# An encoder trunk on one core: the MLP's up product also in Strassen's 2x2 blocks, with its sums of weights formed beside the attention

## Chip, core and metric

One Trainium2 chip, one core. The metric is the device time of one execution in microseconds (us). The kernel computes in float32; products run on TensorE in `float32r` (named fp32r in the rows), where each operand is written as a high part plus a low part and three matmuls (high·high, high·low, low·high: `PASSES`) stand for one exact product.

## What is computed

Two layers over x (1024 tokens by 1024). The attention half of a layer has four groups of heads; the change is in the MLP half and in what stands beside the attention:

```python
h = _rmsnorm(x, norm2_g[l])
u = _dwconv3(h @ w_up[l], conv_w[l], conv_b[l])    # 1024 -> 2 x 2816, a width-3 convolution over the tokens
gate, val = u[..., :D_FF], u[..., D_FF:]
x = x + (jax.nn.silu(gate) * val) @ w_down[l]      # 2816 -> 1024
```

## The kernel before

**Planner and orders.** Python emits the program; a planner then orders every engine's instructions by a timeline of its own. SyncE (SP) issues all DMAs, in one queue. Only in the attention stream is TensorE's order written by hand: `stream` walks numbered positions p (B heads 0 to 63, C 64 to 127, D 128 to 159, A 160 to 223), each with one `step` (L490 splits its transposed probabilities), and calls `fill(p)` to interleave other work: the rest of the input projection up to about p = 55, then `switch` opens the pools of the residual, then output projections of finished head groups (`out_stage`), and at p = 190 pools are closed. `ld` (L438) fetches a head's q, k and v from DRAM some positions ahead, into three buffers.

**MLP up.** The normalised, transposed input lies split in `h2T[0]` and `h2T[1]` (tokens 0 to 511 and 512 to 1023; high and low part; eight chunks of 128 of the inner dimension). The 44 column chunks of `w_up` go in 22 pairs j (gate chunk j, value chunk 22 + j). `load` fetches a chunk of 128x1024 (`rawu`), ScalarE writes its high part, GpSimd its low part (`split`, L132/L136). `product` runs 8 x 3 x 2 = 48 matmuls of 128 columns by 512 tokens into a PSUM tile `u`, so a pair takes 96. `conv` then reads `u` from PSUM: one pass on ScalarE (L939), two on VectorE (L940, L941); `gate` applies silu on ScalarE and multiplies on GpSimd (L948, L952). The first eight products go to DRAM (`gd`), the rest stay in SBUF.

**MLP down.** It is already done by Strassen's seven block products per 2x2 blocks (`DOWN` lists, for each product, the blocks of A = gated values and of B = `w_down` that are added or subtracted, and where the result goes). Each product has 11 steps of 12 matmuls of 512 columns; VectorE forms the sum of A (L1052), `split` makes its two parts, and at the end of a product VectorE adds four PSUM banks into the residual `xacc` (L1061), once for each of 12 uses in all. `prep_down` forms the 77 operands of B for a layer while up runs: two loads, for 55 of them a sum on GpSimd (L1013), a split on ScalarE and VectorE (`wd`), and a store of 512 KB to DRAM (`bd`), from which `down` reads them.

Of the kernel before, what the change touches and what calls it, by code (L numbers as in the profile page):

```python
# [87 lines left out]
GD = 8  # L88


class K:
# [821 lines left out]
    def mlp(self, l, h2T, mp, gd, bd):  # L913


        nc, a = self.nc, self.a
        cw = mp.tile([128, 4, 2 * NFF], F32, tag="cw", name="cw", bufs=1)
# [4 lines left out]
        def load(jj):  # L922
            raw = self.raw.tile([128, KC, 128], F32, tag="raw", name="rawu")
            nc.sync.dma_start(raw, a["w_up"][l, jj])
            w = mp.tile([128, 2, KC, 128], F32R, tag="wu", name="wu", bufs=2)
            self.split((w[:, 0], w[:, 1]), raw, "act", "pool")
            return w

        def product(u, w, halves):
            i = 0  # L930
            for k in range(KC):
                for x, y in PASSES:
                    for n in halves:
                        self.mm(u[:, n * 512:(n + 1) * 512], w[:, x, k, :], h2T[n][:, y, k, :], i == 0, i == 23)
                    i += 1

        def conv(jj, u):
            c = mp.tile([128, S], F32, tag="c", name="c", bufs=3)
            nc.scalar.activation(c, u, AF.Identity, scale=cw[:, 1, jj:jj + 1], bias=cw[:, 3, jj:jj + 1])  # L939
            nc.vector.scalar_tensor_tensor(c[:, 1:], u[:, :S - 1], cw[:, 0, jj:jj + 1], c[:, 1:], op0=ALU.mult, op1=ALU.add)  # L940
            nc.vector.scalar_tensor_tensor(c[:, :S - 1], u[:, 1:], cw[:, 2, jj:jj + 1], c[:, :S - 1], op0=ALU.mult, op1=ALU.add)  # L941
            return c

        def gate(j, us):
            g, v = us
            nc.scalar.activation(g, g, AF.Silu)
            if j < GD:
                nc.gpsimd.tensor_tensor(v, v, g, op=ALU.mult)  # L948
                nc.sync.dma_start(gd[j * 128:(j + 1) * 128, :], v)
                return None  # L950
            t = gp.tile([128, S], F32, tag=f"g{j}", name="gg")
            nc.gpsimd.tensor_tensor(t, v, g, op=ALU.mult)  # L952
            return t.rearrange("p (a c) -> p a c", a=2)

        ws = [load(jj) for jj in (0, NFF)]
        yield
        uu = []
        for w in ws:
            uu.append(self.psS.tile([128, S], F32, tag="S", name="u0"))
            product(uu[-1], w, (0,))  # L960
            yield
        for u, w in zip(uu, ws):
            product(u, w, (1,))
        gs = [gate(0, [conv(jj, u) for jj, u in zip((0, NFF), uu)])]
        gp, pm = yield
        prep = self.prep_down(l, gp, bd)
        for j in range(1, NFF):
            us, w = [], []
            for jj in (j, NFF + j):
                w.append(load(jj))  # L970
                us.append(pm.tile([128, S], F32, tag="u", name="u", bufs=2))
                if j < NFF - 1:
                    product(us[-1], w[-1], (0, 1))
                    us[-1] = conv(jj, us[-1])
                next(prep, None)
                next(prep, None)
            if j == NFF - 1:

                for n in (1, 0):
                    for i in range(2):  # L980
                        product(us[i], w[i], (n,))
                us = [conv(jj, u) for jj, u in zip((j, NFF + j), us)]
            gs.append(gate(j, us))
        yield gs

# [10 lines left out]
    )  # L998

    ORDER = tuple(range(GD // 2, NFF // 2)) + tuple(range(GD // 2))  # L1000

    def prep_down(self, l, gp, bd):

        nc, a = self.nc, self.a
        for n, (_, Bs, _) in enumerate(self.DOWN):
            for c in self.ORDER:
                raw = gp.tile([128, 2, 512], F32, tag="rd", name="rawd", bufs=2)
                for q, (k, j, _) in enumerate(Bs):
                    r0 = (2 * c + k) * 128
# [363 lines left out]
```

## Time and profile before

| | |
|---|---|
| median of 3 runs | 3126.66 us (3122.52 to 3126.93) |
| the profiled execution | 3122.59 us, its span 3120.8 us |
| busy, share of the span | TensorE 95%, weight loads 82%, VectorE 65%, ScalarE 48%, GpSimd 34% |
| DMA | 437.5 MB, mean 140 GB/s |

All rows below come from that one execution. PE is TensorE, DVE is VectorE, ACT is ScalarE, POOL is GpSimd, SPq is SyncE's queue of DMAs. A line number as L132 is that of `split`, a helper, so such rows are told apart by their tiles. Layer 0 runs to about 1570 us, its attention stream from about 200 to 905, its up product to about 1345, its down product to about 1555; layer 1 has the same stages about 1550 us later.

### The profile page before, as it was taken

The numbers are of one execution on the slowest core, as the hardware profiler recorded it, in microseconds if no ns is written. First come the engines' busy times: TensorE is split into PE (matmuls) and PEld (weight loads), VectorE is DVE, ScalarE is ACT, GpSimd is POOL, SyncE is SP. The second block draws the span as 40 slices with busy tenths as digits, with TensorE's granted clock in tenths as the row PEclk, the third lists the DMA queues.
The fourth block names the chain that finished last, engine by engine and source line by source line (L and its number), as shares of the span: only waits on it lengthen the run. The fifth ranks groups of instructions, "written<-read, shape, count | busy, mean of one in ns | idle before, by whom it ended". The sixth has DMA issues, their size and how long they took to land. (4 is left out here: it accounts for less than half of the span.)

```text
span 3120.8 us, 45434 instructions
## 1 busy us (share of the span) xinstructions
PE 2965.2 (95%) x16536; PEld 2551.4 (82%) x16536; DVE 2017.8 (65%) x3366; ACT 1508.5 (48%) x2873; POOL 1049.8 (34%) x902
## 2 busy tenths in 40 slices
PE   7989899899999999999999899998999999999999
PEld 5978888788878888888889788887888788888887
DVE  6778887777744555344666898777777445552455
ACT  5557665766633333222344676657666333332221
POOL 2266410320144554421223653103202445443211
PEclk9999999999999999999999999999999999999999
DMA  4332231332267766355623312313213677662655
GB/s 142 114 105 74 58 122 51 77 73 62 25 221 263 247 231 219 134 211 190 220 96 123 101 54 69 124 45 86 75 45 49 236 272 250 226 214 89 236 193 185
DMA packets 357519, 437.51 MB, mean 140 GB/s; under 512 B 206128, under 2 KB 251568, under 8 KB 357296
## 3 DMA queue, kind: packets, MB, share of 16 engines
q1 hardware_dynamic: 357296, 434.61, 43.8%
q8 instruction: 131, 2.15, 0.3%
q14 instruction: 92, 0.75, 0.1%
HBM read 292.97 MB, written 131.07 MB: 136 GB/s over the span
## 5 line engine op out<-in xcount | busy, mean ns | idle before, releaser
L143 PE MATMUL u<-h2T,wu 128*128 128x512 f32 x4224 | 979.4, 393 | 5.3 <-DVE c L941 5.2
L143 PEld LDWEIGHTS u<-h2T,wu 128*128 128x128 f32 x4224 | 793.0, 188 | 190.1 <-issue 6.9
L143 PE MATMUL pj<-w,hT 128*128 128x256 f32 (+2 forms) x3072 | 488.3, 312 | 21.8 <-ACT w L136 9.6
L143 PEld LDWEIGHTS pj<-w,hT 128*128 128x128 f32 x3072 | 438.5, 194 | 47.2 <-ACT w L136 10.8
L132 DVE TENSOR_TENSOR wd<-rawd,wd 128x512 fp32r<-128x512 f32 x154 | 233.0, 1518 | 233.7 <-ACT wd L136 233.2
L489 ACT CAST PT<-pt 128x512 fp32r<-128x512 f32 x448 | 261.4, 583 | 180.8 <-PE pt L147 172.0
L490 DVE TENSOR_TENSOR PT<-pt,PT 128x512 fp32r<-128x512 f32 x448 | 304.7, 684 | 44.5 <-ACT PT L489 41.9
L147 PE MATMUL pt<-cst,P 128*128 128x128 f32 x1792 | 277.9, 278 | 50.6 <-DVE PT L490 45.0
L940 DVE SCALAR_TENSOR_TENSOR c<-u,cw,c 128x1023 f32<-128x1023 f32 x88 | 112.8, 1282 | 282.7 <-ACT c L939 282.7
L132 POOL TENSOR_TENSOR wu<-rawu,wu 128x1024 fp32r<-128x1024 f32 x88 | 215.1, 2446 | 218.9 <-ACT wu L136 209.7
L143 PEld LDWEIGHTS ot<-PT,v 128*128 128x128 f32 x1664 | 256.9, 193 | 32.2
L147 PEld LDWEIGHTS pt<-cst,P 128*128 128x128 f32 x1792 | 208.8, 142 | 84.1 <-issue 34.2
L143 PE MATMUL ot<-PT,v 128*128 128x256 f32 x1664 | 272.6, 287 | 0.0
L136 ACT CAST wd<-rawd 128x512 fp32r<-128x512 f32 x154 | 95.0, 621 | 348.4 <-POOL rawd L1013 271.8
L1013 POOL TENSOR_TENSOR rawd<-rawd 128x512 f32<-128x512 f32 x110 | 159.6, 1451 | 272.2 <-DMA rawd<-in_w_down_dram 260.5
L939 ACT ACTIVATE c<-u,cw 128x1024 f32<-128x1024 f32 x88 | 106.1, 1206 | 272.1 <-PE u L143 271.9
L143 PE MATMUL d<-h2T,ga 128*128 128x512 f32 x1008 | 230.9, 390 | 0.0
L143 PE MATMUL S<-k,q 96*128 96x512 f32 (+2 forms) x512 | 209.8, 435 | 17.9 <-DVE nmb L655 16.6
L143 PEld LDWEIGHTS d<-h2T,ga 128*128 128x128 f32 x1008 | 189.3, 188 | 40.3
L143 PE MATMUL od<-wo,mT 128*128 128x512 f32 x768 | 200.3, 400 | 0.9 <-DVE mT L1091 0.7
L143 PE MATMUL du<-h2T,ga 128*128 128x512 f32 x792 | 181.4, 390 | 0.0
L143 PEld LDWEIGHTS du<-h2T,ga 128*128 128x128 f32 x792 | 148.7, 188 | 31.7
(216 smaller groups left out, 4529.7 us busy)
## 6 DMA issues: line engine op xcount, KB each, us to landing
bd<-wd SPq DMA_DIRECT2D x154, 512.0 KB, 3.4
h2T<-bd SPq DMA_DIRECT2D x150, 512.0 KB, 3.2
rawd<-in_w_down_dram SPq DMA_DIRECT2D x264, 256.0 KB, 5.1
rawu<-in_w_up_dram SPq DMA_DIRECT2D x88, 512.0 KB, 4.6
rawi<-in_w_in_dram SPq DMA_DIRECT2D x20, 512.0 KB, 3.9
rawo<-in_w_out_dram SPq DMA_DIRECT2D x16, 512.0 KB, 3.3
gd<-c SPq DMA_DIRECT2D x16, 512.0 KB, 5.4
h2T<-gd SPq DMA_DIRECT2D x16, 512.0 KB, 6.8
```

What stands on the lines that cost most here:

```text
L132: eng.tensor_tensor(dst[1], src, dst[0].bitcast(F32), op=ALU.subtract)
L136: self.nc.scalar.copy(dst, src)
L143: self.nc.tensor.matmul(out, l, r, start=start, stop=stop)
L147: self.nc.tensor.transpose(out, in_, self.ident[:p, :p])
L489: nc.scalar.copy(PT[:, 0, :], pt)
L490: nc.vector.tensor_tensor(PT[:, 1, :], pt, PT[:, 0, :].bitcast(F32), op=ALU.subtract)
L939: nc.scalar.activation(c, u, AF.Identity, scale=cw[:, 1, jj:jj + 1], bias=cw[:, 3, jj:jj + 1])
L940: nc.vector.scalar_tensor_tensor(c[:, 1:], u[:, :S - 1], cw[:, 0, jj:jj + 1], c[:, 1:], op0=ALU.mult, op1=ALU.add)
L1013: nc.gpsimd.tensor_tensor(raw[:, 0], raw[:, 0], raw[:, 1], op=ALU.add if Bs[1][2] > 0 else ALU.subtract)
```

## The change

Pairs 3 to 20 of the up product (18 of 22) are done as one 2x2 by 2x2 block product each: rows gate and value, inner dimension in two halves of 512, tokens in two halves. Seven products of 12 matmuls replace eight. Each product of a pair gets a PSUM bank of its own, and VectorE adds the seven banks into two SBUF tiles `g` and `v`, which `conv` now reads from SBUF. Three sums of blocks of the input (`T1`, `T2`, `T4`) are formed in new tiles and one (`T3`) in the place of a quarter of `h2T[1]`, whose contents are put in DRAM (`hd`) first and read back before the last pair.

The weight sums are formed by a new generator `prep`, called from `fill` once per position from p = 66 on, in 91 jobs per layer: 36 for `w_up` (GpSimd adds and subtracts: 1 for an X job, 3 for a Y job, and two stores of 512 KB per pair, `sd`) and 55 for `w_down` (one GpSimd operation, one store of 256 KB, `bd`). `prep_down` and its splits are gone: `down` loads the sums, or `w_down` itself, unsplit and splits them on the spot. The gated products of pairs 0 to 19 all go to DRAM (`gd`); twelve come back into the T tiles, eight into `h2T[1]`.

```diff
-GD = 8
+UP7 = (3, NFF - 1)
...
+    def prep(self, l, pp, sd, bd):
...
+        jobs = [("XY"[i], j) for j in range(UP7[0], UP7[1]) for i in range(2)]
+        jobs += [(n, c) for n, (_, Bs, _) in enumerate(self.DOWN) if len(Bs) > 1 for c in self.ORDER]
...
+            t[i] = pp.tile([128, 2, 512], F32, tag="pw", name="pw", bufs=4)
...
+                nc.sync.dma_start(t[i], a["w_up"][l, jj].rearrange("p (h k) c -> p h (k c)", h=2))
...
+            if kind == "X":
+                G.tensor_tensor(r[:, 0], r[:, 0], r[:, 1], op=ALU.add)
+            elif kind == "Y":
+                x = t[i - 1]
+                G.tensor_tensor(r[:, 0], x[:, 0], r[:, 0], op=ALU.subtract)
+                G.tensor_tensor(x[:, 1], x[:, 1], r[:, 0], op=ALU.subtract)
+                G.tensor_tensor(r[:, 1], r[:, 1], r[:, 0], op=ALU.subtract)
+                nc.sync.dma_start(sd[j, 0], x)
+                nc.sync.dma_start(sd[j, 1], r)
+            else:
+                G.tensor_tensor(r[:, 0], r[:, 0], r[:, 1], op=ALU.add if self.DOWN[kind][1][1][2] > 0 else ALU.subtract)
+                nc.sync.dma_start(bd[kind][j], r[:, 0])
+        for i in range(len(jobs) + 2):
+            if i >= 2:
+                work(i - 2)
+            if i < len(jobs):
+                load(i)
+            yield
...
+        def operand(f, low):
+            w = mp.tile([128, 2, 4, 128], F32R, tag="wu", name="wu", bufs=6)
+            self.split((w[:, 0], w[:, 1]), f, "act", low)
+            return w
...
+        T1, T2, T4 = (tp.tile([128, 2, 4, 512], F32R, tag=f"T{i}", name=f"T{i}") for i in (1, 2, 4))
+        T3 = h2T[1][:, :, 0:4, :]
+        B11, B21, B22 = h2T[0][:, :, 0:4, :], h2T[0][:, :, 4:8, :], h2T[1][:, :, 4:8, :]
+        nc.sync.dma_start(hd, T3.bitcast(F32))
...
+        def sums(k):
+            f = [mp.tile([128, 2, 512], F32, tag="u", name="bf", bufs=2) for _ in range(2)]
+            b11, b12, b22, b21 = f[0][:, 0], f[0][:, 1], f[1][:, 0], f[1][:, 1]
+            for d, t in ((b11, B11), (b12, T3), (b22, B22), (b21, B21)):
+                join(d, t, k)
+            V.tensor_tensor(b11, b12, b11, op=ALU.subtract)
+            V.tensor_tensor(b22, b22, b11, op=ALU.subtract)
+            G.tensor_tensor(b21, b21, b22, op=ALU.subtract)
+            for t, d, eng in ((T1, b11, "dve"), (T2, b22, "dve"), (T4, b21, "pool")):
+                self.split((t[:, 0, k, :], t[:, 1, k, :]), d, "act", eng)
...
+        plain(1, load(1), (0, 1))
+        sums(0)
+        sums(1)
+        plain(2, load(2), (1, 0))
+        sums(2)
+        sums(3)
+        for k in range(4):
+            sums3(k)
...
+            w11 = operand(rg[:, 0:4, :], "pool")
+            s2 = operand(ry[:, 0:4, :], "dve")
+            s1 = operand(rx[:, 0:4, :], "pool")
+            w12 = operand(rg[:, 4:8, :], "dve")
+            s3 = operand(rx[:, 4:8, :], "pool")
+            s4 = operand(ry[:, 4:8, :], "pool")
+            w22 = operand(rv, "pool")
...
+            g, v = (mp.tile([128, S], F32, tag="u", name="u", bufs=2) for _ in range(2))
+            m1 = prod(bank(), w11, B11)
+            nc.scalar.copy(g[:, lo], m1)
+            V.tensor_tensor(v[:, lo], g[:, lo], prod(bank(), s2, T2), op=ALU.add)
+            V.tensor_tensor(g[:, hi], v[:, lo], prod(bank(), s1, T1), op=ALU.add)
+            V.tensor_tensor(g[:, lo], g[:, lo], prod(bank(), w12, B21), op=ALU.add)
+            p = pm.tile([128, S], F32, tag="u", name="X2", bufs=2)
+            m7 = prod(p[:, lo], s3, T3)
+            V.tensor_tensor(v[:, hi], g[:, hi], m7, op=ALU.add)
+            V.tensor_tensor(v[:, lo], v[:, lo], m7, op=ALU.add)
+            V.tensor_tensor(g[:, hi], g[:, hi], prod(p[:, hi], s4, B22), op=ALU.add)
+            p = pm.tile([128, S], F32, tag="u", name="X2", bufs=2)
+            V.tensor_tensor(v[:, lo], v[:, lo], prod(p[:, lo], w22, T4), op=ALU.add)
+            gs = [gate(j, (g, v))]
...
+        ws = load(NFF - 1)
+        nc.sync.dma_start(T3.bitcast(F32), hd)
+        back = [t[:, i, 2 * m:2 * m + 2, :].bitcast(F32) for t in (T1, T2, T4) for i in range(2) for m in range(2)]
...
-    def prep_down(self, l, gp, bd):
...
+                self.split((m[:, 0], m[:, 1]), r, "act", "pool")
...
-                self.split((w[:, 0], w[:, 1]), t[0], "act", "pool" if i % 3 == 1 else "dve")
+                self.split((w[:, 0], w[:, 1]), t[0], "act", "dve")
...
+                if 66 <= p < 190:
+                    adv("prep", 1)
```

`sums3(k)` forms `T3` in place: two joins on VectorE, a subtraction on GpSimd, a split whose low part alternates between GpSimd and VectorE. `prod` is 4 x 3 matmuls into one bank. `plain` is a pair as before, with the token halves one after the other.

## Rows read from the trace of the kernel before

**Rows 1.** Stretches: busy us of each engine (x instructions), granted clock, DMA share, GB/s.
```profile
950.00:1300.00 350.00, 350.00 (x1518) 284.50 (x1517) 178.08 (x125) 118.61 (x138) 180.56 (x92) 1.00 0.68 231
1350.00:1550.00 200.00, 200.00 (x876) 164.09 (x875) 109.93 (x148) 47.46 (x79) 37.09 (x28) 1.00 0.63 223
408.00:640.00 232.00, 212.14 (x1435) 187.25 (x1435) 176.19 (x358) 154.51 (x346) 41.55 (x31) 0.99 0.32 87
```

**Rows 2.** Chain that ended last, layer 1's MLP: start us, us, what, matmuls.
```profile
2417.81 11.03 PE u L143 x48
...
2493.29 411.39 PE u L143 x1776
2904.68 29.92 PE d L143 x132
```

**Rows 3.** Waits of TensorE, whole span: us in total, times, longest.
```profile
PE u L143 <- DVE c L941: 5.2, 3, 2.5
```

**Rows 4.** Groups by form: busy us, mean ns of one, idle before, releaser.
```profile
L941 DVE SCALAR_TENSOR_TENSOR c<-u,cw,c 128x1023 f32<-128x1023 f32 x88 | 112.8, 1282 | 3.0
L132 DVE TENSOR_TENSOR w<-raw,w 128x512 fp32r<-128x512 f32 x16 | 10.7, 695 | 1.1 <-ACT w L136 0.9
L1061 DVE TENSOR_TENSOR xacc<-xacc,d 128x512 f32<-128x512 f32 x56 | 35.1, 679 | 9.9 <-PE d L143 9.9
L136 ACT CAST wd<-rawd 128x512 fp32r<-128x512 f32 x154 | 95.0, 621 | 348.4 <-POOL rawd L1013 271.8 <-DMA rawd<-in_w_down_dram 74.8 <-issue 1.6
L939 ACT ACTIVATE c<-u,cw 128x1024 f32<-128x1024 f32 x88 | 106.1, 1206 | 272.1 <-PE u L143 271.9
```

**Rows 5.** VectorE's instructions in order of time, up stage: start us, us, what.
```profile
1062.95 2.26 DVE L132 TENSOR_TENSOR wd<-rawd,wd 128x512 fp32r<-128x512 f32 x1 [0.85 <-ACT wd L136]
1068.46 0.69 DVE L132 TENSOR_TENSOR wd<-rawd,wd 128x512 fp32r<-128x512 f32 x1 [3.26 <-ACT wd L136]
...
1071.89 1.28 DVE L941 SCALAR_TENSOR_TENSOR c<-u,cw,c 128x1023 f32<-128x1023 f32 x1
1073.64 2.25 DVE L132 TENSOR_TENSOR wd<-rawd,wd 128x512 fp32r<-128x512 f32 x1 [0.46 <-ACT wd L136]
```

**Rows 6.** GpSimd's instructions in the same time.
```profile
1062.21 2.44 POOL L132 TENSOR_TENSOR wu<-rawu,wu 128x1024 fp32r<-128x1024 f32 x1
...
1071.66 1.29 POOL L1013 TENSOR_TENSOR rawd<-rawd 128x512 f32<-128x512 f32 x1 [3.88 <-DMA rawd<-in_w_down_dram]
1072.91 2.44 POOL L132 TENSOR_TENSOR wu<-rawu,wu 128x1024 fp32r<-128x1024 f32 x1
1075.30 1.75 POOL L1013 TENSOR_TENSOR rawd<-rawd 128x512 f32<-128x512 f32 x1
1077.01 2.41 POOL L952 TENSOR_TENSOR gg<-c 128x1024 f32<-128x1024 f32 x1
```

**Rows 7.** Stretch 1352 to 1360, columns as in rows 1.
```profile
1352.00:1360.00 8.00, 8.00 (x37) 6.56 (x36) 5.36 (x5) 4.72 (x7) 1.31 (x1) 1.00 1.02 413
```

**Rows 8.** VectorE's L490 alone (one per position) by stretch: busy us (x times).
```profile
408.00:640.00 232.00, 62.72 (x93) 0.99 0.32 87
640.00:840.00 200.00, 52.81 (x78) 0.99 0.19 51
```

**Rows 9.** DMA issues, 404 to 424 us: times, KB each, median us to landing.
```profile
xacc<-in_x_dram SPq DMA_DIRECT2D x8, 512.0 KB, 7.5
...
ld<-sC SPq DMA_DIRECT2D x1, 256.0 KB, 6.8
```

**Rows 10.** DMA issues, 408 to 640 us.
```profile
ld<-sC SPq DMA_DIRECT2D x3, 256.0 KB, 3.5
```

**Rows 11.** DMA issues on the page: loads of the weights.
```profile
rawd<-in_w_down_dram SPq DMA_DIRECT2D x264, 256.0 KB, 5.1
rawu<-in_w_up_dram SPq DMA_DIRECT2D x88, 512.0 KB, 4.6
```

**Rows 12.** Line 1010 (loads of `prep_down`) in layer 0: first and last start.
```profile
L1010 SPq DMA_DIRECT2D rawd<-in_w_down_dram x132: 328/472/1311, 867.7 to 1268.1; - x132
```

## Forecast

> **What bounds the kernel now.** I read the page's shares first, then the stretches, because a share is a mean over stages. In the up stretch and in the down stretch TensorE is busy for the whole of the time, at a granted clock of 1.00 (2.4 GHz), while VectorE is busy for about half and GpSimd for half and a fifth [rows 1]. The chain says the same from its end: it is nothing but matmuls from the up product to the last step [rows 2]. Of all the waits of TensorE, the up product's longest group is 5.2 us in the whole span, three waits for VectorE to free PSUM [rows 3]. So a matmul less in up is time less, unless the work that replaces it becomes the bound; and the sums, splits and stores of `prep_down`, which run beside it, cost nothing today, so that taking them out of up gains nothing by itself. The stretch 408 to 640 us is most of C and D of the attention, where the new sums will run: TensorE is busy 212 of 232 us, VectorE 176, GpSimd 42, and the DMA engines 0.32 [rows 1].
>
> **Change, part by part.** The sum is made against the profiled execution, 3122.6 us; the median of the runs is 4 us above it, and I forecast the median by the same offset, rounded. A difference under 0.2% is about what cannot be told from no change.
>
> *Matmuls.* A pair goes from 96 to 84, so 36 pairs lose 432. The chain has 411.39 us for 1776 in up, 231.6 ns each, and 29.92 us for 132 in down, 226.7 ns [rows 2]. Up alternates two banks with the token halves; the new `prod` stays in one bank with the three passes of down's form. The second half of the first pair already runs one token half at a time: 11.03 us for 48, 229.8 with the drain of the last in it. So I take 226.7: 36 x (96 x 0.2316 - 84 x 0.2267) = 36 x (22.23 - 19.04) = -115. Two more pairs per layer get separate halves: 4 x 96 x 0.0049 = -2. If the form does not matter, it is -432 x 0.2316 = -100. Both ends stay for the range.
>
> *What else a new pair asks of the engines in its 19.04 us.* ScalarE: seven casts of 0.62, two conv passes of 1.21, silu at most as much, one copy at most a cast: 4.3 + 2.4 + 1.2 + 0.6 = 8.5 [rows 4]. VectorE: seven adds with one PSUM operand at 0.68, four conv passes at 1.28, two low parts at 0.69 when alone: 4.8 + 5.1 + 1.4 = 11.3 [rows 4, 5]. GpSimd: five low parts of 512 columns at 1.29 and the gate product at 2.41: 8.9 [rows 6]. None reaches 19.04 alone. But VectorE and GpSimd hold each other up: a `wd` took 2.26 us when it began beside a GpSimd subtraction that ran to 1064.65, and ended 0.56 us after that; alone it took 0.69; the GpSimd sum at 1075.30 took 1.75 where it met a `wd` that ran to 1075.89. The conv pass at 1071.89, which reads `u` from PSUM, took its 1.28 across two GpSimd instructions [rows 5, 6]. So it is operations with two SBUF inputs that collide, and the change turns the four conv passes of a pair into such ones. Colliding work per pair is then 5.1 + 2 x 0.6 + 8.9 = 15.2 us of 19.04; with the seven adds in no overlap at all it is 20.0. TensorE runs up to a pair ahead of VectorE, since each of the seven products has its own bank, so bursts don't matter and the mean does. I take 0 here, with 0 to 36 x 0.96 = 35 as the bounds.
>
> DMA falls: a pair moves 2.36 MB in 19.04 us, 124 GB/s, where up moves 231 GB/s today [rows 1]. The store of a gated product waits on SP for GpSimd, and the next loads are queued behind it; but six operand slots for seven operands let the first tile of the next pair be fetched nearly a pair ahead of its use, so a store that is some us late is covered by 19 us of matmuls. Without that cover it would be a landing of 4.6 us [rows 11] per pair. I take 0.
>
> The Trainium skill, SBUF — State Buffer, section "SBUF: two separate sides", says that GpSimd and a VectorE instruction with two SBUF inputs share one pair of ports as an exclusive lock: whoever starts first keeps it for the whole instruction and the other blocks. It speaks against moving conv's input into SBUF. The trace agrees (2.26 beside, 0.69 alone). By the rule the sum would be as above, +0; by GpSimd instructions that each block all of VectorE it would be the 35.
>
> *Forming T1 to T4.* Per layer VectorE has 8 operations for each `sums(k)` and 2.5 for each `sums3(k)`, so 42, at 0.64 (back to back) 27 us; GpSimd 2 and 1.5, so 14 at 1.29: 18 us. In the same time GpSimd splits pairs 1, 2 and part of 3 (11 x 1.29) and makes three gate products: 21 us. That is 66 colliding us, and three pairs' conv from PSUM, 15 us, besides. TensorE covers it with half of pair 0, pairs 1 and 2, and pair 3 up to the product that takes T3: 48 + 192 + 48 = 288 matmuls, 65 us. Late next would be that product. Bounds 0 and 81 - 65 = 16 per layer; most overlaps, so I take 4: +8.
>
> *The end of up.* T3's place is read back, 2.1 MB, at 413 GB/s [rows 7] 5 us, when its last reader is done; 24 matmuls and a token half of the last pair (48) lie in front of its first use, 16 us. Twelve loads of 0.52 MB compete. I take 0.
>
> *Down.* A step has 12 matmuls, 2.72 us. VectorE now splits A in every step and GpSimd B: colliding, 2 x 0.64 + 1.29 = 2.57 in 55 steps and 1.93 in 22, and 48 adds into `xacc` at 0.68 [rows 4]: 217 us if all is in a row, against 77 x 2.72 = 209. Bounds 0 and 8 per layer; weights run six steps ahead, and I take 2: +4.
>
> *Sums beside the attention.* Per layer 18 x 4 + 55 = 127 GpSimd operations at 1.29, 164 us, and DMAs of 72 x 0.524 + 165 x 0.262 = 81 MB. The pool opens at about p = 55, not 66: the planner doesn't keep to the place in the program. It issued the eight reloads of x, written one per position from 66 on, together at about 408 us [rows 9], and began `prep_down` at 868 us, while the attention stream still ran [rows 12]. From 408 us (93 of C's and D's steps to 640, 78 to 840 [rows 8], so p = 53) to p = 190 at 640 + 44 x 2.56 = 753 us there are 345 us. GpSimd needs 164 + 42 to 640 and little more; the DMA engines 81 MB / 413 GB/s = 196 us beside a third of their time taken. So it fits, but DMA is saturated for some 270 us, and VectorE has little there with two SBUF inputs (the probabilities and scores come from PSUM). What it costs is latency: with the reloads of x in flight a load of a head took 6.8 us where it takes 3.5 [rows 9, 10]. Queued behind such a load on SP are the next head's and the copies that D's keys need; three loads of C (in the program two positions, 5 us, ahead of the first transpose) and four pairs of copies of D are exposed, 7 x 3.3 = 23 us per layer if each comes through whole. Half of them will have slack: 10 per layer, +20. Lower bound 0; the upper one is a rival.
>
> *Sum:* 3122.6 - 117 + 0 + 8 + 0 + 4 + 20 = 3037.6; with the offset, 3040.
>
> **Rivals.** (a) *SP holds the attention back.* SP issues in one order, and a store waits on it for GpSimd's sum. If the loads of heads stand behind stores that come later than planned, the attention goes at the pace of the jobs: two loads in flight, so a pair of `w_up` jobs takes a landing and the Y job's three operations, 4.6 + 3.9 = 8.5 us, and two `w_down` jobs 5.1 + 1.3 = 6.4 [rows 6, 11]: 18 x 8.5 + 55 x 3.2 = 329 us for what the positions 53 to 159 pass in 232 + 13 x 2.56 = 265. That is +64 per layer in place of +10: 3148, slower. It decides from +53 per layer in the attention: 3040 - 20 + 2 x 53 is 3126. For it: six us of landing are already more than the lead of a load. Against it: four buffers, and a planner that put loads well ahead. (b) *VectorE and GpSimd bound the new pairs* at 20.0 us, 35 more: 3075. For it, the collisions of rows 5 and 6 at twice today's number of VectorE operations; against it, that `wd` collides in the same way today and TensorE hardly waits [rows 3], and that the adds from PSUM don't collide. It cancels the gain only from 22.3 us per pair. (c) *The matmuls keep up's spacing* of 231.6 ns: 17 us less gain, 3057. (d) *Nothing but the matmuls counts*, the whole latency of the attention's loads being slack: 3122.6 - 117 + 4 = 3010.
>
> **Chances.** Forecast 0.66 (with (c), which only shifts it; its own range 3012 to 3068), (b) 0.12, (a) in part or whole 0.16, (d) 0.06. Half of (a) lies under 3115 us. The range 3008 to 3112 leaves out the worse half of (a) and the tails, some 0.14. Faster by over 0.2%: 0.66 + 0.12 + 0.06 and a little under half of (a), 0.07, in all 0.91; I give 0.06 of it to what no row of before can show and say 0.85; within 0.2%, 0.04; slower 0.11.
>
> **What would show it.** Up: chain of waits all matmuls, a new pair of 19.0 us, about 227 ns per matmul; VectorE at 60 to 85% of it, conv passes of 1.28 up to 2.5 us. Wrong if TensorE waits there for VectorE's adds or GpSimd's low parts by over 1 us per pair. Start of up: one wait of a few us before T2 or T3's product. Down: steps of 2.7 us. Attention: GpSimd at 70% and DMA near 0.9 from 408 to 680 us, the stretch to the start of up 10 us longer per layer, TensorE waiting for loads of heads and copies of keys; the prediction falls if that stretch grows by 50.

## The result: slower by 1%, and the profile after

The changed kernel takes 3159.16 us (median of 4 runs, 3154.85 to 3161.71); the kernel before, in the same comparison, 3126.8 (3122.52 to 3127.81). The ratio is 1.0105, with a 95% interval of 1.0087 to 1.0122: slower by some 32 us, where 3040 was forecast and 3112 was the end of the range. The profiled run has a span of 3157.0 us, 36.2 more than before, and a mean clock of 0.964 for 0.988.

The first table is cut at events that both kernels have: first and last `PT` subtraction of a layer's attention (VectorE, line 490), first matmul of `u` behind it (pair 0), first and last matmul of `d`. All times are differences of their starts in the two profiled runs, in us.

| stage | before, layers 0 and 1 | after | difference |
|---|---|---|---|
| start to attention | 208.6 | 211.2 | +2.6 |
| attention | 627.6, 627.2 | 652.5, 661.4 | +24.9, +34.2 |
| attention to up | 26.3, 26.3 | 40.3, 39.8 | +14.0, +13.5 |
| up | 494.5, 495.5 | 461.3, 460.8 | -33.2, -34.7 |
| down | 211.3, 209.2 | 211.3, 209.3 | 0.0, +0.1 |
| layer change | 187.2 | 202.6 | +15.4 |

The differences add up to +36.8. So up did become shorter, and four other places took back more than it gave.

The stretches of the kernel after that answer to those of [rows 1], columns as there (the down product starts some us later now, so its stretch is 1370 to 1570):

```profile
950.00:1300.00 350.00, 345.57 (x1495) 282.44 (x1494) 209.80 (x227) 143.33 (x198) 178.60 (x112) 0.99 0.33 117
1370.00:1570.00 200.00, 200.00 (x876) 164.09 (x875) 159.56 (x169) 82.03 (x143) 102.12 (x74) 1.00 0.33 106
408.00:640.00 232.00, 202.33 (x1308) 178.10 (x1307) 165.22 (x312) 141.39 (x307) 149.72 (x116) 0.94 0.91 298
```

Up and down look as the forecast had them: TensorE has no gap but two waits of 3.4 and 1.0 us at pair 2 and at the first new pair, while VectorE forms the sums `T`; VectorE stands at 60 and 80% of the stretch, GpSimd at 51%. The attention has DMA at 0.91 of the time instead of 0.32, and 1308 matmuls in the 232 us that held 1435.

VectorE's two conv passes of that up stretch, grouped by line (busy us, mean ns of one, idle before). The first pass kept its 1281 ns, the second took 1745 where [rows 4] have 1282; the stretch above shows that it cost TensorE nothing:

```profile
L976 DVE SCALAR_TENSOR_TENSOR c<-u,cw,c 128x1023 f32<-128x1023 f32 x36 | 61.6, 1745 | 0.1
L975 DVE SCALAR_TENSOR_TENSOR c<-u,cw,c 128x1023 f32<-128x1023 f32 x36 | 44.8, 1281 | 25.6 <-ACT c L974 13.8 <-DMA rawy<-sd 11.8
```

TensorE's waits over the whole span of the kernel after (what it waited for, us in total, times, longest), the main ones that are new or grew:

```profile
PE u L143 <- ACT wu L136: 28.1, 2, 14.2
PE ntp L147 <- POOL nx L165: 23.8, 2, 12.4
...
PE S L143 <- DMA k<-k: 15.4, 6, 6.7
...
PE S L143 <- DMA kl<-kl: 11.6, 7, 3.5
...
PE u L143 <- DVE c L976: 6.9, 2, 3.4
PE ntp L147 <- DVE nx L167: 6.5, 1, 6.5
```

The same two waits for the copies of D's keys in the kernel before:

```profile
PE S L143 <- DMA kl<-kl: 2.4, 4, 0.7
...
PE S L143 <- DMA k<-k: 0.9, 2, 0.5
```

The first line is the end of up (the last pair's operands) and the second the end of the attention (a norm's product on GpSimd), each once per layer. The next two are D's copies, `u <- c` is pair 2 behind the first sums `T`, once per layer, and the last is the layer change. (The kernel before has one wait with the last line's name too, 9.9 us, but at the start of the program; at its layer change there is none.) All but pair 2 got experiments.

### The profile page after: what moved, and what is told of

The parts are those of the page before. It is cut to its first block, busy times and chain, and to the rows that moved or that the text cites. A ratio compares the mean times of both kernels' runs of the same rounds, so it can differ in the third digit from the quotient of the medians.

```text
span 3157.0 us, 46345 instructions
## 1 busy us (share of the span) xinstructions
PE 2902.1 (92%) x16104; PEld 2507.3 (79%) x16104; DVE 2235.6 (71%) x3676; ACT 1623.3 (51%) x3137; POOL 1490.9 (47%) x1296
## 5 line engine op out<-in xcount | busy, mean ns | idle before, releaser
L143 PE MATMUL pj<-w,hT 128*128 128x256 f32 (+2 forms) x3072 | 494.9, 315 | 23.6 <-ACT w L136 13.6
L143 PE MATMUL X<-h2T,wu 128*128 128x512 f32 x1728 | 413.0, 391 | 1.9 <-ACT wu L136 1.9
L143 PEld LDWEIGHTS X<-h2T,wu 128*128 128x128 f32 x1728 | 324.3, 188 | 73.2 <-ACT wu L136 2.8
L490 DVE TENSOR_TENSOR PT<-pt,PT 128x512 fp32r<-128x512 f32 x448 | 304.7, 685 | 62.7 <-ACT PT L489 60.6
L143 PE MATMUL X<-T,wu 128*128 128x512 f32 x1296 | 314.8, 392 | 0.0
L143 PEld LDWEIGHTS X<-T,wu 128*128 128x128 f32 x1296 | 243.3, 188 | 54.1
L143 PEld LDWEIGHTS ot<-PT,v 128*128 128x128 f32 x1664 | 258.5, 194 | 32.6 <-ACT os L515 0.3
L143 PE MATMUL S<-k,q 96*128 96x512 f32 (+2 forms) x512 | 213.7, 442 | 31.0 <-DMA k<-k 15.4
L143 PE MATMUL d<-h2T,ga 128*128 128x512 f32 x1056 | 241.9, 390 | 0.0
L132 POOL TENSOR_TENSOR h2T<-h2T 128x512 fp32r<-128x512 f32 x110 | 150.1, 1367 | 157.2 <-ACT h2T L136 157.2
L143 PE MATMUL u<-h2T,wu 128*128 128x512 f32 x768 | 186.6, 405 | 35.2 <-ACT wu L136 28.1
L143 PEld LDWEIGHTS u<-h2T,wu 128*128 128x128 f32 x768 | 149.4, 196 | 70.8 <-ACT wu L136 28.9
L948 POOL TENSOR_TENSOR pw<-pw 128x512 f32<-128x512 f32 x110 | 140.6, 1284 | 105.8 <-DMA pw<-in_w_down_dram 93.5
L655 DVE CUSTOM_DVE_ANT_0 P<-S,toep 128x1024 f32<-128x1024 f32 x128 | 155.4, 1217 | 26.7 <-PE pt L147 23.7
```

What stands on the lines that cost most here:

```text
L132: eng.tensor_tensor(dst[1], src, dst[0].bitcast(F32), op=ALU.subtract)
L143: self.nc.tensor.matmul(out, l, r, start=start, stop=stop)
L490: nc.vector.tensor_tensor(PT[:, 1, :], pt, PT[:, 0, :].bitcast(F32), op=ALU.subtract)
L655: nc.vector.tensor_tensor_reduce(out=P, in0=Ps["S", i, s], in1=self.toep[:, o:o + S], scale=-slope, scalar=-NEG, op0=ALU.add, op1=ALU.min, ...
L948: G.tensor_tensor(r[:, 0], r[:, 0], r[:, 1], op=ALU.add if self.DOWN[kind][1][1][2] > 0 else ALU.subtract)
```

## Experiments

Times are medians; "ratio" is to the kernel before on the same chip, with its 95% interval. Stage lengths are cut as in the table, from one profiled execution each. In the five runs that leave the attention's program alone (experiments 3, 4, 6 and the first two of 9 to 11) it took 651 to 655 us in layer 0 and 658 to 667 in layer 1, so differences of a few us there say nothing by themselves.

**1. Without the sums** (two jobs a layer are kept; up and down read other rows of the same size).

```
-        jobs = [("XY"[i], j) for j in range(UP7[0], UP7[1]) for i in range(2)]
-        jobs += [(n, c) for n, (_, Bs, _) in enumerate(self.DOWN) if len(Bs) > 1 for c in self.ORDER]
+        jobs = [("X", 3), ("Y", 3)]
```

> Leaves out all sums of weight blocks but two per layer: their loads, adds and stores beside the attention go, and the up and down stages read other rows of the same size in their place, so the transfers and matmuls of the two products stay. Theory (the sums beside the attention lengthen it): from the first score product to the last the layers take 627 us again instead of 652.5 and 661.4, and the time falls by 25 + 34 us to about 3100 us, while the gap ahead of the up product (14 us a layer), the one at its end (14 a layer) and that at the layer change (15) stay. Rival (the attention is longer for another reason, such as a place in the order of the work that the new up product took): 652 and 661 stay, about 3159 us.

3104.68 us, ratio 0.9925 (0.9909 to 0.9942). The attention took 631.0 and 632.5 us; the other three places stayed (40.6 and 40.6 ahead of up, 204.3 at the change). The sums cost the attention 21.5 and 29 us, and the whole run is 54 us shorter without them.

**2. The sums' transfers alone** (their GpSimd operations are left out; one of three places shown).

```
             else:
-                G.tensor_tensor(r[:, 0], r[:, 0], r[:, 1], op=ALU.add if self.DOWN[kind][1][1][2] > 0 else ALU.subtract)
                 nc.sync.dma_start(bd[kind][j], r[:, 0])
```

> Leaves out the GpSimd operations of the sums (1, 3 or 1 for each job); their loads and stores stay, so the stored rows are not sums. Theory (it is the transfers: the copies of the keys of the last group of heads wait among them): the attention stays at 652 and 661 us, the time within 5 us of 3159. Rival (it is GpSimd's time, or the lock between it and VectorE): the attention takes 627 us again, about 3100 us. If both have a part, between.

3137.85 us, ratio 1.0034 (1.0021 to 1.0047); attention 643.1 and 649.3. Between the two: 9.4 and 12.1 us go with GpSimd's operations, some 40% of the loss, and the rest stays with the transfers. TensorE's waits for the copies `k<-k` were not shorter here (10.7 us from 400 to 750 us, 6.6 in the kernel after). What did change is the clock: for the same 3989 or so matmuls of a layer's attention TensorE was busy 580.0 and 587.0 us, 3.9 and 6.9 less than in the kernel after, at a granted clock of 0.97 and 0.96 in place of 0.96 and 0.94. The other 5.5 and 5.2 us are idle time that went.

**3. Gate products out of `raw`**: that of pair 20 goes to `ry`, that of pair 21 stays in its conv tile.

```
-            t = self.raw.tile([128, S], F32, tag="raw", name="gg")
+            t = mp.tile([128, S], F32, tag="ry", name="gg", bufs=1) if j == NFF - 2 else v
```

> The gate products of the last two pairs are kept in other tiles, so both buffers of the pool raw are free at the end of the up product and through the down product. Theory (one raw buffer alone makes the last pair's second weight tile late, and the next layer's first weights too): the layer change, from the last down matmul to the next layer's first score product, falls from 202.6 to about 187 us, and the up product's end by about 5 us a layer (the wait for a raw buffer was 5.4 us; the wait of SP behind the reads of w_down rows stays): 3159 - 15 - 10 = 3134 us. Rival (SP's order decides: the store of the residual rows stands ahead of the next layer's loads whatever buffers are free): the layer change stays at 200 us or more, and the time falls by no more than 10 us, to 3149 us or above.

3136.88 us, ratio 1.0031 (1.0017 to 1.0045). Up fell to 444.4 and 443.4 us, by 16.9 and 17.4, more than the 5 expected; the layer change stayed at 203.9. So the theory is right about the end of up and wrong about the change. SP's queue and TensorE at the end of up in the kernel after (start us, us, what, times):

```profile
1333.23 1.52 SPq L1151 DMA_DIRECT2D rb<-in_w_down_dram  x2
1334.81 9.48 SPq L995 DMA_DIRECT2D rawu<-in_w_up_dram  x2
```

```profile
1341.38 3.99 PE L143 MATMUL u<-h2T,wu 128*128 128x512 f32 x8 [13.92 <-ACT wu L136]
```

and SP in this run:

```profile
1302.75 3.09 SPq L995 DMA_DIRECT2D rawu<-in_w_up_dram  x2
```

The last pair's weights go out 32 us earlier. In the kernel after, one of the two buffers of `raw` is kept for `gg`, and the loads stand behind reads for the down product that wait for VectorE. The stretch 1300 to 1350 us, after and in this run:

```profile
1300.00:1350.00 50.00, 35.94 (x149) 28.60 (x148) 21.31 (x27) 14.20 (x20) 17.06 (x11) 0.86 0.59 226
```

```profile
1300.00:1350.00 50.00, 50.00 (x220) 41.00 (x219) 29.27 (x30) 21.03 (x28) 23.59 (x15) 1.00 0.85 319
```

A wait of 14 us costs 17. Behind it, from 1342 to 1347 us, 16 matmuls ran at a granted clock of 0.71, where the full clock holds 22 in 5 us; that is 1.4 us more, and the rest of the difference is not accounted for.

**4. Pair 1's low parts on VectorE.**

```
-            ws = []
+            ws, low = [], "dve" if j == 1 else "pool"
...
-                ws.append([operand(raw[:, 4 * h:4 * h + 4, :], "pool") for h in range(2)])
+                ws.append([operand(raw[:, 4 * h:4 * h + 4, :], low) for h in range(2)])
```

> The low parts of pair 1's operands, and of these alone, are formed by VectorE instead of GpSimd. Theory (in GpSimd's queue two of them, which wait for a late load, stand in front of the norm's multiply): the stretch from the last score product to the first up matmul falls from 40 to about 27 us in both layers, and the time by 26 us to 3133 us. Rival (the late loads hold VectorE's queue in the same way, or the norm waits for something else): the stretch stays at 36 us or more, the time above 3150 us.

3171.95 us, ratio 1.0146 (1.0129 to 1.0163); ahead of up still 41.0 and 41.8. The theory fell. (The four runs span 3159.82 to 3174.55 and the profiled one is the fastest; what made the others slower than the kernel after is not shown.) GpSimd in the kernel after had seemed to say it: two low parts stand in front of the norm's product (line 165), with 11.80 us of waiting:

```profile
893.28 2.49 POOL L132 TENSOR_TENSOR wu<-rawu,wu 128x512 fp32r<-128x512 f32 x2 [11.80 <-ACT wu L136]
895.73 2.35 POOL L165 TENSOR_TENSOR nx<-nx,gn 128x1024 f32<-128x1024 f32 x1
```

But ScalarE in this run has the high parts of the same operand in front of the norm's scaling (line 164), waiting for the load:

```profile
891.38 1.14 ACT L136 CAST wu<-rawu 128x512 fp32r<-128x512 f32 x2 [11.49 <-DMA rawu<-in_w_up_dram]
892.42 1.15 ACT L164 ACTIVATE nx<-xacc,nr 128x1024 f32<-128x1024 f32 x1
```

Whichever engine splits the weights stands still. What is late is the load, and SP's queue in the kernel after shows where it stands: behind 11.5 us of issuing the convolution weights and behind a load for pair 3.

```profile
872.41 7.83 SPq L964 DMA_DIRECT2D cw<-in_conv_w_dram  x3
880.28 3.70 SPq L965 DMA_DIRECT2D cw<-in_conv_b_dram  x1
884.08 3.64 SPq L1074 DMA_DIRECT2D rawy<-sd  x1
887.82 0.38 SPq L995 DMA_DIRECT2D rawu<-in_w_up_dram  x1
```

The kernel before issues the convolution weights in the same place and for as long (7.99 and 3.71 us from 844.95 on) and pays nothing for it: there GpSimd has the norm's products at 855.25 and 863.00 and the next split of weights only at 884.57. So it takes both, a late load and a split of it that was set ahead of the norm.

**5. The convolution weights early** (their four loads are written where the sums begin, into a tile that is held for the whole program).

```
-        cw = mp.tile([128, 4, 2 * NFF], F32, tag="cw", name="cw", bufs=1)
...
+        cw = self.cw
...
```

> The four loads of the convolution weights, which hold SP's queue for 11.7 us ahead of pair 1's weights, go out in the middle of the attention instead, into a tile of their own. Theory (after the run with VectorE's low parts: whichever engine splits pair 1's weights stands in its queue ahead of the norm, and the split waits for a transfer that SP issues late): the weights are issued about 10 us earlier, and the stretch from the last score product to the first up matmul falls from 40 to about 28 us in both layers, the time to about 3135 us. Rival (the raw buffers or pair 3's first load, which was put ahead, hold pair 1's weights anyway): the stretch stays at 36 us or more, the time at 3150 us or more.

3148.76 us, ratio 1.0072 (1.0051 to 1.0093). Ahead of up: 29.9 and 28.9 us, as the theory has it. But the planner put layer 0's loads at 13.76 us of the program, in front of the first input weights, and the start grew from 211.2 to 225.1 us; layer 0's attention was 665.8, 13 us longer, for a reason that was not looked for. The first three loads held SP for 10.1 us there.

**6. Residual stores issued later** (behind the first input projection of layer 1, in the program).

```
-                    nc.sync.dma_start(xd[t * 128:(t + 1) * 128, :], xt)
...
+                if l:
+                    for t in range(NT):
+                        nc.sync.dma_start(xd[t * 128:(t + 1) * 128, :], xacc[:, t, :])
```

> The stores of the residual rows at the start of layer 1 are issued behind the first input projection instead of one ahead of each row's norm. Theory (SP's queue: a store that waits 26 us for VectorE stands ahead of the gain row that the first norm needs, and of the input weights): the layer change falls from 202.6 to about 187 us, the time to about 3144 us. Rival (the first norm waits for the last additions into the residual, or for the input weights, whatever SP does): the change stays at 199 us or more, the time at 3155 us or more.

3160.64 us, ratio 1.0111 (1.0079 to 1.0142); change 203.9. No answer to the question: the planner put the stores ahead of the gain row's load again. SP in the kernel after, where they wait for the last additions of the down product:

```profile
1546.15 3.07 SPq L1144 DMA_DIRECT2D h2T<-bd  x2
1575.69 1.01 SPq L1312 DMA_DIRECT2D xd<-xacc  x2
1576.80 0.52 SPq L1314 DMA_DIRECT2D gn<-in_norm_g_dram  x1
```

**7. D's copies early.**

```
-        self.stack(g - 12, qt, 64, [(0, 64, q, 0)], [(0, 64, q, q, 64)])
-        self.stack(g - 9, kt, 64, [(0, 64, k, 0)], [(0, 64, k, kl, 0)], [(k, 0, 64, 64), (kl, 0, 64, 64)])
+        self.stack(g - 14, qt, 64, [(0, 64, q, 0)], [(0, 64, q, q, 64)])
+        self.stack(g - 12, kt, 64, [(0, 64, k, 0)], [(0, 64, k, kl, 0)], [(k, 0, 64, 64), (kl, 0, 64, 64)])
```

> In the last group of heads to have its own key copies (D) the query stack is made two positions earlier and the key stack, with its two copies, three. Theory (what the transfers of the sums cost there is the latency of these copies and the slower clock after each wait): TensorE's waits for the key copies, 10.9 us in layer 0 and 16 in layer 1, fall under 2 us a layer, and the attention by 10 to 20 us a layer, to about 638 and 645 us; the time to about 3130 us. Rival (the copies are only what is seen; the sums slow the attention through many small delays, GpSimd's among them): the attention falls by less than 6 us a layer, the time stays above 3147 us.

3109.13 us, ratio 0.9936 (0.992 to 0.9953). The attention took 633.1 and 633.2 us, 19.4 and 28.2 less, with every sum and every transfer still there: all but 2.1 and 0.7 us of what experiment 1 gained by leaving them out. TensorE in the kernel after, where it meets the copies (start us, us, what, the idle time before):

```profile
600.80 0.63 PE L143 MATMUL o<-cst,os 128*128 128x64 f32 x4 [0.98 <-DVE PT L490]
604.90 0.58 PE L143 MATMUL S<-k,q 128*128 128x256 f32 x1 [3.48 <-DMA k<-k]
608.45 0.58 PE L143 MATMUL S<-kl,q 128*128 128x256 f32 x1 [2.96 <-DMA kl<-kl]
608.82 0.42 PE L143 MATMUL S<-k,q 128*128 128x256 f32 x1
609.04 0.41 PE L143 MATMUL S<-kl,q 128*128 128x256 f32 x1
```

and the time of the copies from 590 to 620 us, from issue to landing (KB, us), after and then before:

```profile
k<-k SPq DMA_DIRECT2D x1, 256.0 KB, 7.8
kl<-kl SPq DMA_DIRECT2D x1, 256.0 KB, 9.1
```

```profile
k<-k SPq DMA_DIRECT2D x2, 256.0 KB, 3.8
kl<-kl SPq DMA_DIRECT2D x2, 256.0 KB, 4.2
```

These two copies take 7.8 and 9.1 us among the transfers of the sums, and were issued too near to their use. Over 560 to 660 us the medians are 5.8 and 7.3 us, against 3.7 and 4.1 before; in this run, where the copies go out earlier, they also land sooner, in 4.3 and 5.8. The stretch 600 to 650 us before, after and in this run:

```profile
600.00:650.00 50.00, 44.68 (x363) 41.73 (x362) 40.55 (x123) 36.97 (x100) 20.54 (x12) 1.00 0.37 85
```

```profile
600.00:650.00 50.00, 35.17 (x230) 32.75 (x231) 26.55 (x80) 24.66 (x70) 32.62 (x23) 0.80 0.97 267
```

```profile
600.00:650.00 50.00, 43.88 (x351) 40.15 (x351) 39.81 (x122) 36.59 (x104) 32.83 (x22) 1.00 0.86 247
```

230 matmuls in place of 363, then 351 again: the waits for copies are 27 us in both layers together, and taking them away gave 48. The other 20 us are TensorE's clock, 0.80 around them and 1.00 without. The attention of layers 0 and 1 shows it, after and in this run: of the 19.4 and 28.2 us, idle time of TensorE makes 13.6 and 14.1, and 5.9 and 14.1 are busy time that the same matmuls no longer need.

```profile
211.20:863.70 652.50, 583.83 (x3989) 527.47 (x3988) 510.50 (x967) 414.94 (x861) 317.02 (x293) 0.96 0.61 190
1779.20:2440.60 661.40, 593.86 (x3995) 536.17 (x3994) 505.62 (x962) 414.85 (x861) 319.14 (x293) 0.94 0.59 188
```

```profile
211.10:844.20 633.10, 577.98 (x3989) 520.29 (x3988) 504.39 (x967) 413.89 (x861) 318.44 (x293) 0.98 0.62 196
1761.20:2394.40 633.20, 579.72 (x3989) 521.00 (x3988) 506.55 (x964) 413.19 (x861) 319.36 (x293) 0.97 0.63 196
```

**8. Experiments 3, 5, 6 and 7 together.**

> Four edits together: the gate products of the last two pairs out of the raw buffers (34 us less in the two up products when made alone), the early convolution weights, the later residual stores and the earlier key copies. If each gives what its theory says and the gains add up: 3159 - 34 - 24 - 15 - 28 = about 3058 us, faster than the kernel before by 2.2%. If the convolution weights and the key copies give nothing, as their rivals have it, about 3110 us; if the gaps only move elsewhere, 3120 us or more.

3061.42 us, ratio 0.979 (0.9766 to 0.9815). Up 439.5 and 440.1, ahead of it 29.1 and 28.9, attention 639.9 and 636.3; the start 221.5 and the change 203.6, near to what they were in their own runs. The gains add up: 97.7 us together, against 81.2 for the four one by one.

**9 to 11. The layer change.** A one-element copy behind each norm puts the stores behind the gain row's load; another order of the tags in the pool puts the operands `wu` at its end; and both in one kernel with 3, 7 and the convolution weights in the residual's pool.

```
+                if l:
+                    nc.vector.tensor_copy(xt[:, 0:1], xt[:, 0:1])
+                    nc.sync.dma_start(xd[t * 128:(t + 1) * 128, :], xt)
...
```

```
+        for tag, n in (("u", 2), ("c", 3)):
+            mp.tile([128, S], F32, tag=tag, name=tag, bufs=n)
...
```

> A one-element copy in each residual row behind its norm makes the store of that row depend on the norm, so that the gain row's load stands ahead of all those stores in SP's queue (in the run before, the stores stood ahead of it still). Theory 1 (SP's order alone holds the next layer back): the load goes out before 1560 us, the layer change falls from 202.6 to about 187 us, the time to 3144 us. Theory 2 (the pool of the up stage grew over the place of the next layer's gain row and norm tiles, and what lies there is the operands that TensorE reads up to the last down matmul): the load still goes out at 1570 us or later, when the last operands have been read, and the change stays at 198 us or more, the time at 3155 us or more.

> The pool of the up stage is laid out in another order: tiles that the down product leaves early come first, where the next layer's gain row and norm tiles will lie, and the operands last. The order of SP's queue stays. Theory 2 alone (the place is what holds the load, not the stores ahead of it): the layer change falls to about 187 us, the time to 3144 us. If both must go (the store that waits for the last additions stands ahead): it stays at 198 us or more, as in the run with the copies, and only the two together bring it down.

> The gate products out of the raw buffers, the early key copies, the convolution weights loaded early but into the residual's pool (in the run before they were put at the very start of the program, where they cost 10 to 14 us), the stores behind the norms, and the operands last in the pool. If the parts add up: 3061 us of the run with four edits, less the 10 us at the start, less 15 at the layer change: about 3036 us. If the layer change stays, 3051 us; if the early weights still cost what they cost at the start, 3046 us or more.

The stores behind the norms: 3147.26 us, ratio 1.0067 (1.0047 to 1.0088), change 196.5, 6 us less. The order of the pool: 3155.42, ratio 1.0094 (1.0075 to 1.0112), change 203.0. All five: 3060.45, ratio 0.9788 (0.9774 to 0.9801), change 199.8, attention 644.8 and 648.1. In the first of them SP issues the gain row 5.0 us ahead of the last down matmul (1567.88 and 1572.9), in the last 27 us ahead of it (1507.35 and 1534.3), yet TensorE's wait for the first norm only falls from 6.5 to 5.6 and 4.3 us: SP then stands at the input weights until 1536.34, behind the last down matmul. So the stores are one part, worth 6 us alone and 3 in the run with all five. An earlier gain row is worth little more, and the order of the pool gave no time, alone or with the stores.

**12 to 14. The buffers of the weights, and short loads.** The low-rank weights of C, which take both buffers of `raw` early, are loaded behind the first projection; and the convolution weights are laid out in DRAM as they lie in SBUF, so that two short loads do (the arrays are laid out ahead of the program, outside the measured time).

```
+        nc.sync.dma_start(cw[:, 0:3, :], a["conv_w"][l])
+        nc.sync.dma_start(cw[:, 3, :], a["conv_b"][l])
...
```

> Gate products out of the raw buffers, early key copies, stores behind the norms, and the convolution weights laid out in DRAM as they lie in SBUF, so that two short loads take the place of four that hold SP's queue for 11.7 us. Theory (the run with five edits paid in the attention, 645 and 648 us, for the 11 us that the early weights hold SP's queue there): with the short loads the attention takes 633 to 636 us, the stretch ahead of the up product 29 us, the layer change 197 us, the time about 3042 us. Rival (the attention of that run was longer for another reason, the layout of the pool): the attention stays at 640 us or more, the time at 3055 us or more.

> Stores behind the norms, operands last in the pool, and the two low-rank weights of group C loaded behind the first projection, so that they don't hold the two raw buffers. Theory (the layer change is held by a chain of three: the stores ahead, then the place of the gain row, then the raw buffers, held by weights whose tiles lie where the down product still reads): with all three gone the change is 187 us, the time 3144 us. Rival (other reuse of the up stage's place, the norm tiles and the weight tiles, holds it too): 195 us or more, as with the stores alone.

> All of these together. If the layer change comes down to 187 us: about 3032 us; if it stays at 197 us: 3042 us.

With three edits at the change (stores behind the norms, the order of the pool, the low-rank weights later): 3139.91 us, ratio 1.0042 (1.003 to 1.0055), change 192.8: 10 of the 15 us. SP there:

```profile
1554.84 0.42 SPq L1318 DMA_DIRECT2D gn<-in_norm_g_dram  x1
...
1569.51 0.98 SPq L182 DMA_DIRECT2D raw<-in_w_in_dram  x2
```

The gain row goes out 12.7 us ahead of the last down matmul (1567.5), while further input weights still wait until it is done. The layer change in the kernel before, after and in this run shows what the 15 us consist of:

```profile
1568.30:1755.50 187.20, 175.03 (x1087) 159.42 (x1086) 126.54 (x343) 95.87 (x250) 74.99 (x108) 1.00 0.35 108
```

```profile
1576.60:1779.20 202.60, 182.07 (x1081) 163.87 (x1080) 141.32 (x367) 106.13 (x268) 81.78 (x119) 0.95 0.38 116
```

```profile
1567.50:1760.30 192.80, 177.96 (x1085) 161.78 (x1084) 133.28 (x366) 97.28 (x253) 75.28 (x109) 0.98 0.38 118
```

TensorE was idle 8.4 us more than before, 6.5 of them in the wait for the first norm, and 7.0 us longer busy with the same work, at a granted clock of 0.95 instead of 1.00. The three edits leave 2.7 us of the first and 2.9 of the second; the wait for the first norm is still 4.3 us there. What holds that norm was not tried, nor which of the two edits beside the stores gave the last 4 us.

Three of the edits (3, 7, and the stores behind the norms) with the short loads: 3053.01, ratio 0.976 (0.9745 to 0.9776), attention 632.0 and 635.5, ahead of up 32.6 and 31.6. SP there needs 0.9 us for the convolution weights:

```profile
849.82 0.47 SPq L963 DMA_DIRECT2D cw<-in_conv_w_dram  x1
850.34 0.43 SPq L964 DMA_DIRECT2D cw<-in_conv_b_dram  x1
```

So it was the early convolution weights that made the attention of the run with five edits long, and not the pool's order, which the run with all six shares and which is short too. All six: 3046.26, ratio 0.9741 (0.9723 to 0.9759), attention 628.2 and 635.6, up 443.8 and 443.4, change 193.8. TensorE's waits for the copies, for the last pair and for the norm on GpSimd are gone from the head of its list:

```profile
PE pt L147 <- DVE PT L490: 44.0, 55, 2.8
PE ntp L147 <- DVE nx L167: 15.0, 3, 10.5
PE stp L147 <- DVE kl L466: 12.2, 8, 4.5
PE S L143 <- DVE nmb L655: 12.0, 6, 5.0
```

So the kernel with the Strassen up product and six repairs is 2.6% faster than the kernel before. In its profile up is 50.7 and 52.1 us shorter than there, and no other stage is shorter by more than 1 us: the gain comes out of up, and the other stages still take back 27 us of it. What the repairs that have nothing to do with the new product, such as the short loads, would give the kernel before was not run.

## Why the prediction was wrong

**Right in the main: the matmuls and what they need.** In the steady new pairs, ScalarE's copy of the first product (line 1089) comes every 19.24 us, 15 pairs between these two:

```profile
1011.28 0.57 ACT L1089 COPY u<-X 128x512 f32<-128x512 f32 x1
...
1299.96 0.57 ACT L1089 COPY u<-X 128x512 f32<-128x512 f32 x1
```

That is 229 ns for each of 84 matmuls (229 in layer 1 too), halfway between the forecast's 226.7 and rival (c)'s 231.6. So (c) is half right. An old pair took 22.16 us in layer 0 and 22.24 in layer 1 (from silu to silu, line 946 of the kernel before, 1305.95 to 1328.11 and 2853.34 to 2875.58), so a pair saves some 2.96 us, 107 in all, where -115 was forecast and -100 by (c). Why the new form does not reach down's 226.7 is not shown. Without the gap at its end (experiment 3) up is 50.1 and 52.1 us shorter than before, 102 in all, where the matmuls' term less T1 to T4 was -109. TensorE waited 1.9 us for operands in all new pairs, so VectorE and GpSimd don't bound them: rival (b) is out, though the second conv pass did stretch, to 1.75 us. (Its break-even of 22.3 us per pair left out the other terms; with 85 us of gain over 36 pairs it is 21.4.) The start of T cost a wait of 3.4 us per layer, with 4 forecast. Down was forecast at +4 and gave 0.

**Mis-sized: the sums beside the attention.** The mechanism was named, the copies of D's keys among saturated DMA, but 10 us a layer were taken and 21.5 and 29 measured (experiment 1). The step that failed is "7 x 3.3 = 23 us per layer if each comes through whole. Half of them will have slack": TensorE's waits for the copies came to 10.9 and 16.1 us, not far from the 10 taken, but each wait was priced as its own length, with none of the slower clock around it, which was 20 of the 48 us that experiment 7 gave back. Rival (a), SP at the pace of the jobs, is not what happened: it was to add 64 us a layer, and three positions more of lead took the loss away with all jobs in place.

**Failed: "The end of up. ... I take 0."** It weighed only the reading back of T3 and the twelve loads against 16 us of cover. The loss is 16.9 and 17.4 us, from a resource that the step didn't look at: `gg` takes one of the two buffers of `raw`, and the last pair's own weights are late.

**Missing from the sum: two places.** Ahead of up, +14 and +13.5: the planner set pair 1's splits ahead of the last norms on ScalarE and GpSimd, and there they wait for a load that SP issues behind the convolution weights (experiments 4 and 5). That it could do so because there are now six operand slots, each half as big, in place of two is likely, but no run put the old slots back. At the layer change, +15.4: the residual's stores ahead of the gain row are 6 us of it alone; the place of the pool and the raw buffers were the other suspects, and clearing both beside the stores gave 4 us more, not told apart. The prediction spoke of queues for what it moved, but costed neither what the wider buffers let the planner move, nor what memory and buffers the grown stage keeps from the next one.

In one line, in us: -102.2 up, +34.3 its end, +59.1 attention, +27.5 ahead of up, +15.4 change, +2.6 start, +0.1 down: +36.8, where -117 + 8 + 4 + 20 = -85 had been forecast.

What stays open: why TensorE's wait for the copies stayed in experiment 2 while the clock rose and other idle time went, and what holds the first norm in the last 5 us of the layer change.

## What to carry to other kernels

Work put beside a stage with idle engines still makes that stage's transfers slower: look for each transfer whose consumer is close behind, and give it more lead before filling the DMA queues; here three positions were worth 48 us. When a change widens a pool, adds slots or parks a result in a shared buffer, list what is loaded next into that pool, into that buffer, and, since the planner reuses memory, into the same addresses a stage later; and list what an in-order queue can now take ahead of time. A split that waits for its load blocks every engine that takes part in it, so moving half of it from one engine to another changed nothing here; moving the load ahead did.

## What the runs showed of the hardware

A gap on TensorE can cost more than its length. Around and behind waits of 3.48 and 2.96 us the granted clock was 0.52 (604 to 609 us) and 0.55 (609 to 615), so mostly at the lower of its two levels, and the score matmuls of 128x256 behind the second wait took 0.42 and 0.41 us, where those of the position before took 0.29 and 0.28. A wait of 14 us cost 17, and waits of 27 us in sum cost 48, 20 of them as busy time at the lower clock.

Copies of 256 KB inside SBUF landed in 3.7 and 4.1 us (medians from 560 to 660 us) in the kernel before, where the DMA engines were busy 0.39 of that time, and in 5.8 and 7.3 in the kernel after, at 0.94. Issued earlier, in experiment 7, they took 4.3 and 5.8 at 0.91.

Four loads of the convolution weights, with 4-byte elements in a strided order, hold SP's queue for 11.5 us; in a layout that matches SBUF they are two loads and take 0.9.
